# Decay rows in sample state homes, deferred outputs and a down tile in two banks in a decoder-trunk kernel

## The chip, the cores and the metric

The kernel runs on one core of one Trainium2 chip. The metric is the device time of one execution in microseconds (us). Before the change it is 991.7 us, the median of three runs (991.33 to 992.5).

The engines are called as in the profile: PE (TensorE, matmuls; PEld are its weight loads), DVE (VectorE), ACT (ScalarE), POOL (GpSimd), and SP (SyncE), which here only issues DMAs. A line number such as L928 is a line of the kernel before.

## The reference

One inference step of a decoder trunk: an FFN taken at half weight, a mixer, and a second FFN at half weight, each behind an RMS norm and with a residual add, then a last RMS norm. There are 512 prompt tokens and 8 sample tokens, 520 columns in all, and the model dimension is 1024. All data is float32.

```python
h = h + 0.5 * swiglu(rms_norm(h, n1), wg1, wu1, wd1)          # FFN dimension 2816
m, ... = mixer(rms_norm(h, nm), ...)
h = h + m
h = h + 0.5 * swiglu(rms_norm(h, n2), wg2, wu2, wd2)
y = rms_norm(h, final)
```

The mixer projects to a pooling part, a gate z, and x, B, C and dt of a Mamba-2 state-space scan (SSD). x, B and C go through a causal convolution over four tokens and SiLU. The scan works in chunks of 128 tokens, per head (16 heads in 2 groups, head size 64, state size 128):

```python
Acs = cumsum(dt * A)                                          # within a chunk
decay = exp(mask(Acs[l] - Acs[s]))
y_diag = (C[l] . B[s]) * decay * dt[s] * x[s]                 # summed over s
states = B[s] * exp(Acs[-1] - Acs[s]) * dt[s] * x[s]          # summed over s
y_off = C[l] . h_prev * exp(Acs[l])
y = y_diag + y_off + d_skip * x
```

The sample tokens read and update given states. Besides the two outputs y, the new pooling, convolution and SSD states are returned.

## The kernel before, in words

**Layout.** The 1024 features lie in eight tiles of 128 partitions with 520 columns each; a matmul takes half of the columns (260). To keep float32 precision each product is three matmuls of rounded parts, high by high, high by low, low by high (`mm3`, L116 to L121). A weight unit is loaded by SP, ACT casts the high part (L107), DVE subtracts for the low part (L108).

**FFN.** FFN1's down projection ends with `down` (L352 to L392): for each of the eight output tiles d it multiplies into a pair of PSUM banks (tag `BE`, two such pairs), and `done` takes both halves out with one DVE instruction (L369), adds them to h (L376) and calls `after`, which prepares that tile of the mixer's input (ACT L138, DVE L139, square and sum L149, L150). Tag `A` is two single banks that the gate and up products use.

**Mixer.** PSUM is then given anew as eight single banks (`bank`). The mixer opens with the `dt` product (L636 to L642), which goes over the two halves and, inside, over the eight input tiles. Its work is then cut into steps that two strings order, `CONV_PLAN` and `GATE_PLAN` (L39 to L46): b and x are projections with convolution (`conv`, L698), p, c and m the pooling (projection and window sums, `centre` L751, `mix` L760), A and B the two halves of a chunk step, z the gate's projections (`zproj`), s the sample tokens, e the stores of the small states (`outs_a`), o, G, H, g and h the gating and the output projection.

There are eight chunk steps: the four chunks of head group 0, then those of group 1, so A4 is chunk 0 of group 1, "the fifth". `ssd_a` (L860) does this for one step: it transposes B (`pb`) and four tiles of x (`px`, L871) on PE; loads the step's eight rows of cumulated decay from DRAM, each spread over 128 partitions (`ab`, L873, 512 KB); POOL makes `we`, the decay to the chunk's end (L877), and ACT its exponential (L878); for later chunks ACT makes `E`, the exponential of the rows (L883), and `cd` (L885); ACT (L888) and DVE (L890) subtract for four heads each, ACT exponentiates (L892, L893), all in place, and DVE multiplies with the masked scores `scm` (L899). DVE makes `xdt`, x times the step size dt, out of the bank `px` (L895), and POOL `xw` (L898). `ssd_b` (L902) multiplies (`yo`, `pst`, `yd`), brings the state up to date (`hst`, L920 and L921), adds up (L924, L925) and writes the output into x (L928, four instructions).

**Buffers.** `ab` has three buffers, `E`, `cd`, `xdt` and `we` two. Tag `h0` is four buffers of 2 KB per partition: first `dv` and `bct`, later the sample states that `sample` (L809) loads ("sample state homes").

**What sets the order.** A planner orders each engine's instructions at build time: it plays the program against modelled durations, and gives an engine, among the instructions that are ready by the model, the one traced first. `tc.high_priority()` puts what is traced inside ahead of others; `tc.issue_after(i)` keeps what is traced inside behind instruction i on i's engine; `tc.keep_in_program_order` pins an instruction behind what was traced before it on its engine. On the chip each engine then runs its list strictly in order, SP's DMA issues too, and waits by semaphore for data and for buffers and banks to come free.

## Time and profile before

| what | value |
|---|---|
| median of three runs | 991.7 us |
| profiled execution, its own time | 992.8 us |
| profiled execution, its span (first to last instruction) | 991.0 us |
| PE busy | 969.8 us |
| DVE busy | 800.0 us |
| ACT busy | 552.8 us |
| POOL busy | 87.4 us |
| read from HBM, written | 105.86 MB, 7.34 MB |

The profile is one execution. A row of a timeline gives the start in us from the span's start, the duration in us, the engine, the line, the operation, the names of what it writes and reads (`out<-in`), shapes, and how many instructions the row merges (x). In brackets stands how long the engine was idle before it, and which engine, name and line ended that. Where several semaphores were waited for, the one that came last is named. A matmul's end is modelled and overlaps the next one's start, so the distance of two starts is the better measure. By the core's rows, FFN1 ends and the mixer begins near 366 us, and the chunk steps lie between 426 and 561.

### The profile page before, as it was taken

The page shows a single profiled execution, that of the slowest core. Times are in us where ns is not written, and L with a number is a line of the kernel's source. Part 1 is how long each engine was busy: PE and PEld are TensorE (multiplying, and loading weights), DVE is VectorE, ACT ScalarE, POOL GpSimd, SP SyncE. Part 2 cuts the span into 40 slices and gives each one's busy share as a digit, 9 for nine tenths or more (in the row PEclk, how much of TensorE's full clock was granted, in tenths as well). Part 3 has the DMA queues.
Part 4 walks back from the last instruction along what each step waited for, and adds up shares of the span by engine and source line. Part 5 has one row for each costly group of instructions (what it writes and reads, how often), then busy time and mean ns, then how long its engine had stood idle before and what let it go on. Part 6 is the DMA issues. An engine that isn't in the chain of part 4 may idle for free.

```text
span 991.0 us, 19414 instructions
## 1 busy us (share of the span) xinstructions
PE 969.8 (98%) x7852; PEld 951.0 (96%) x7852; DVE 800.0 (81%) x1295; ACT 552.8 (56%) x1011; POOL 87.4 (9%) x157
## 2 busy tenths in 40 slices
PE   7999999999999999999999999999999999999996
PEld 6899999999999999999899999899999999999995
DVE  7999656997569688788978997999967899668876
ACT  7566414664136455685668574666643566534653
POOL 0000000000000000156522000100013000120000
PEclk9999999999999999999999999999999999999998
DMA  6332322323222232262335232323246423363212
GB/s 188 121 128 95 120 86 86 128 86 129 85 86 81 91 126 85 82 206 100 124 114 186 81 125 86 113 98 128 100 117 198 162 88 127 120 181 119 96 65 87
DMA packets 42027, 114.48 MB, mean 116 GB/s; under 512 B 6408, under 2 KB 13512, under 8 KB 41936
## 3 DMA queue, kind: packets, MB, share of 16 engines
q1 hardware_dynamic: 38864, 103.78, 30.6%
q0 software_dynamic: 3072, 9.44, 3.7%
q8 instruction: 62, 1.02, 0.4%
q14 instruction: 29, 0.24, 0.1%
HBM read 105.86 MB, written 7.34 MB: 114 GB/s over the span
## 4 chain that ended last, share of the span: by engine, by line
PE 90%; DVE 5%; POOL 1%; DMA 1%; issue 1%; ACT 1%; SPq 0%; DVEq 0%; ACTq 0%
PE A L121 8%; PE A L117 8%; PE A L120 8%; PE dn L121 7%; PE dn L117 7%; PE dn L120 7%; PE BE L117 6%; PE BE L121 6%; PE BE L120 6%; PE wo L117 2%; PE wo L121 2%; PE wo L120 2%; PE P L234 2%; PE inz L117 2%; PE inz L121 2%; PE inz L120 2%
## 5 line engine op out<-in xcount | busy, mean ns | idle before, releaser
L117 PE MATMUL dn<-g,whi_1d 128*128 128x260 f32 x352 | 99.3, 283 | 0.2 <-DVE td L369 0.2
L120 PE MATMUL dn<-g,whi_1d 128*128 128x260 f32 x352 | 99.5, 283 | 0.0
L121 PE MATMUL dn<-g,wlo_1d 128*128 128x260 f32 x352 | 99.4, 283 | 0.0
L369 DVE SCALAR_TENSOR_TENSOR td<-dn,r_f 128x520 f32<-128x520 f32 x40 | 27.8, 698 | 72.7 <-PE dn L121 72.7
L121 PE MATMUL dn<-g,wlo_2d 128*128 128x260 f32 x256 | 72.5, 283 | 0.8 <-DVE wlo_2d L108 0.8
L117 PE MATMUL dn<-g,whi_2d 128*128 128x260 f32 x256 | 72.3, 282 | 0.0
L120 PE MATMUL dn<-g,whi_2d 128*128 128x260 f32 x256 | 72.3, 282 | 0.0
L117 PEld LDWEIGHTS dn<-g,whi_1d 128*128 128x128 f32 x352 | 66.1, 188 | 0.4 <-DVE td L369 0.4
L120 PEld LDWEIGHTS dn<-g,whi_1d 128*128 128x128 f32 x352 | 66.3, 188 | 0.0
L121 PEld LDWEIGHTS dn<-g,wlo_1d 128*128 128x128 f32 x352 | 66.2, 188 | 0.0
L299 ACT COPY ac<-A 128x260 f32<-128x260 f32 x123 | 45.6, 374 | 28.9 <-PE A L121 28.0
L107 ACT CAST whi_1d<-raw_1d 128x1024 fp32r<-128x1024 f32 (+1 forms) x24 | 23.5, 981 | 67.0 <-PE dn L120 54.2
L262 DVE TENSOR_TENSOR s<-raw 128x1024 f32<-128x1024 f32 x41 | 49.9, 1218 | 5.6 <-DMA raw<-in_w2gu 5.6
L234 PE MATMUL P<-xg_f,raw 128*128 128x260 f32 x192 | 45.4, 392 | 6.4 <-ACT sq_f L157 5.5
L121 PEld LDWEIGHTS dn<-g,wlo_2d 128*128 128x128 f32 x256 | 48.2, 188 | 1.0 <-DVE wlo_2d L108 1.0
L234 PEld LDWEIGHTS P<-xg_f,raw 128*128 128x128 f32 x192 | 36.9, 196 | 12.2 <-ACT sq_f L157 5.4
L117 PEld LDWEIGHTS dn<-g,whi_2d 128*128 128x128 f32 x256 | 48.3, 189 | 0.0
L120 PEld LDWEIGHTS dn<-g,whi_2d 128*128 128x128 f32 x256 | 48.2, 188 | 0.0
L117 PE MATMUL wo<-catg,whi_wo 128*128 128x260 f32 x128 | 37.2, 290 | 0.0
L117 PE MATMUL inz<-xh_mx,whi_inz 128*128 128x260 f32 x128 | 36.8, 287 | 0.1
L117 PE MATMUL inx<-xh_mx,whi_inx 128*128 128x260 f32 x128 | 36.4, 284 | 0.0
L121 PE MATMUL wo<-catg,wlo_wo 128*128 128x260 f32 x128 | 36.2, 283 | 0.0
(1341 smaller groups left out, 3936.7 us busy)
## 6 DMA issues: line engine op xcount, KB each, us to landing
raw<-in_w2gu SPq DMA_DIRECT2D x44, 512.0 KB, 4.5
raw<-in_w1gu SPq DMA_DIRECT2D x42, 512.0 KB, 4.5
raw_1d<-in_w1d SPq DMA_DIRECT2D x16, 512.0 KB, 4.5
raw_2d<-in_w2d SPq DMA_DIRECT2D x16, 512.0 KB, 4.4
raw_wo<-in_w_out SPq DMA_DIRECT2D x12, 512.0 KB, 4.9
ab<-scr_acs SPq DMA_DIRECT2D x8, 512.0 KB, 4.9
h<-in_state_ssm SPq DMA_DIRECT2D x16, 256.0 KB, 3.7
raw_inz<-in_w_in SPq DMA_DIRECT2D x8, 512.0 KB, 3.8
```

What stands on the lines that cost most here:

```text
L107: nc.scalar.copy(h, src)
L117: first = nc.tensor.matmul(ps, whi, xhi, start=start, stop=False, **kw)
L120: nc.tensor.matmul(ps, whi, xlo, start=False, stop=False, **kw)
L121: nc.tensor.matmul(ps, wlo, xhi, start=False, stop=stop, **kw)
L234: nc.tensor.matmul(self.banks[f, u][b][:, :HB], ws(self.raw[f][:, u], j + 4 * q), xg[:, slot[q]], start=j == q == 0, stop=j == 3 and q == ...
L262: nc.vector.tensor_tensor(out=s1, in0=diag, in1=up0, op=ALU.add)
L299: nc.scalar.copy(keep, out[:, :HB])
L369: nc.vector.scalar_tensor_tensor(out=t, in0=banks[d][:, :, :HB], scalar=-0.5, in1=self.nx[3].rearrange("p (b t) -> p b t", b=2), op0=ALU.mult,
```

## The change

What it does, part by part:

- The last down tile of FFN1 (d = 7) multiplies into two single banks of tag `A` instead of a pair of tag `BE`, and is taken out half by half, at high priority (`done_by_half`). The `dt` product goes over the input tiles outside and the halves inside.
- The rows of the fifth step (chunk 0 of group 1) go into two buffers of tag `h0`, four heads each, with two DMAs of 256 KB. The lists of heads (`G`) and the products with `scm` follow.
- In every step, `xdt` is traced behind the transposes, at high priority. `we` is made on DVE instead of POOL, for the fifth step in two instructions. `E` and `cd` have three buffers.
- The output of step B1 (`ssd(1)`) is put off to a new step `Y1` behind A3, kept behind A3's `xdt` on DVE. Step `c3` moves behind B2, also kept behind A3's `xdt`.
- The stores of the small states (`e0`) move from the end of `CONV_PLAN` behind A5, and are kept behind A5's load of rows on SP.

```diff
-    "c3 X1 m2 A3 B2 e0"
+    "X1 m2 A3 Y1 B2 c3"
...
-    "A4 z0 B3 z1 m3 z2 B4 z3 s2 A5 z4 s2 B5 ...
+    "A4 z0 B3 z1 m3 z2 B4 z3 s2 A5 e0 z4 s2 B5 ...
...
+                    if after is not None and d == KD - 1:
+                        banks[d] = [ps[0].tile([P, 512], F32, tag="A", bufs=2, name=f"dn{self.i}_{d}_{c}{b}")
+                                    for b in range(2)]
...
+            def done_by_half(d):
+                for b, hs in enumerate(HALVES):
+                    t = self.wx.tile([P, 2, HB], F32, tag="tg", bufs=2, name=f"td{self.i}_{d}_{c}{b}")[:, b]
+                    nc.vector.scalar_tensor_tensor(out=t, in0=banks[d][b][:, :HB], scalar=-0.5, in1=self.nx[3][:, hs],
+                                                   op0=ALU.mult, op1=ALU.mult)
+                    nc.vector.tensor_tensor(out=h[:, d, hs], in0=t, in1=h[:, d, hs], op=ALU.add)
+                    after(d, b, hs)
...
-    for b, hs in enumerate(HALVES):
-        for k in range(KD):
+    for k in range(KD):
+        for b, hs in enumerate(HALVES):
...
+        if (c, g) == (0, 1):
+            abs_ = [mp.tile([P, 4, P], F32, tag="h0", bufs=4, name=f"ab{c}{g}{i}") for i in range(2)]
+            ab = None
+        else:
+            ab = mp.tile([P, 8, P], F32, tag="ab", bufs=3, name=f"ab{c}{g}")
+            abs_ = [ab]
+        n = 8 // len(abs_)
+        for i, t in enumerate(abs_):
+            r0 = c * NH + 8 * g + n * i
+            held["ab"] = nc.sync.dma_start(out=t, in_=scr_acs[r0 : r0 + n].unsqueeze(0).to_broadcast([P, n, P]))
...
+        xdt = mp.tile([P, 8, 64], F32, tag="xdt", bufs=2, name=f"xdt{c}{g}")
+        with tc.high_priority():
+            held["xdt"] = nc.vector.tensor_tensor(out=xdt, in0=px.rearrange("p (a b) -> p a b", a=8),
+                                                  in1=dtc.unsqueeze(2).to_broadcast([P, 8, 64]), op=ALU.mult).ins
...
-        nc.gpsimd.tensor_tensor(out=we, in0=ab[:, :, CH - 1], in1=atc, op=ALU.subtract)
+        for i, t in enumerate(abs_):
+            s = slice(n * i, n * i + n)
+            nc.vector.tensor_tensor(out=we[:, s], in0=t[:, :, CH - 1], in1=atc[:, s], op=ALU.subtract)
...
-            E = mp.tile([P, 4, P], F32, tag="E", bufs=2, name=f"E{c}{g}")
+            E = mp.tile([P, 4, P], F32, tag="E", bufs=3, name=f"E{c}{g}")
...
+        for t in abs_:
+            nc.vector.tensor_tensor(out=t, in0=t, in1=scm.unsqueeze(1).to_broadcast([P, n, P]), op=ALU.mult)
...
+        if (c, g) == ssd(1):
+            held["out"] = out
+        else:
+            out()
+
+    def ssd_out(_):
+        with tc.issue_after(held["xdt"]):
+            held.pop("out")()
...
     def outs_a():
+        with tc.issue_after(held["ab"].ins):
+            for name, t in (("ncp", ncp), ("ncs", sconv), ("npp", npp), ("nps", spool)):
+                nc.sync.dma_start(out=outs[name], in_=t)
+
+    def centre(j):
+        with tc.issue_after(held["xdt"]) if j == 3 else nullcontext():
+            pooled[j][0]()
```

More of the change, by code (lines that the diff above doesn't have):

```diff
@@ L358, in part @@
                     units[d] = load_unit(ins[f"w{self.i}d"][d, :, lo * P : hi * P], n * P, f"{self.i}d{d}_{c}")
-                    banks[d] = ps[0].tile([P, 2, 512], F32, tag="BE", bufs=2, name=f"dn{self.i}_{d}_{c}")
+                    if after is not None and d == KD - 1:
+                        banks[d] = [ps[0].tile([P, 512], F32, tag="A", bufs=2, name=f"dn{self.i}_{d}_{c}{b}")
+                                    for b in range(2)]
+                    else:
+                        t = ps[0].tile([P, 2, 512], F32, tag="BE", bufs=2, name=f"dn{self.i}_{d}_{c}")
+                        banks[d] = t[:, 0], t[:, 1], t
                 wh, wl = units[d]
@@ L368, in done @@
                 hd = h[:, d].rearrange("p (b t) -> p b t", b=2)
-                nc.vector.scalar_tensor_tensor(out=t, in0=banks[d][:, :, :HB], scalar=-0.5,
+                nc.vector.scalar_tensor_tensor(out=t, in0=banks[d][2][:, :, :HB], scalar=-0.5,
                                                in1=self.nx[3].rearrange("p (b t) -> p b t", b=2), op0=ALU.mult,
@@ L391, in down @@
                 part(d, range(n))
-                done(d)
+                if after is not None and d == KD - 1:
+                    with tc.high_priority():
+                        done_by_half(d)
+                else:
+                    done(d)
         def down_by_half(self, c, lo, after, wd):
@@ L914, in ssd_b @@
             nc.tensor.matmul(yd[64 * (q % 2) : 64 * (q % 2) + 64, (q // 2) * P : (q // 2 + 1) * P], xdt[:, q],
[L915 removed]
+                             G[q], start=True, stop=True)
         if c == 0:
@@ L926, in ssd_b, with out @@
             yr = E
-        for q in range(4):
-            nc.vector.scalar_tensor_tensor(out=X[:, 4 * g + q, cs], in0=X[:, 4 * g + q, cs],
-                                           scalar=v("d_skip", 4 * g + q), in1=yr[:, q], op0=ALU.mult, op1=ALU.add)
+        def out():
+            for q in range(4):
+                nc.vector.scalar_tensor_tensor(out=X[:, 4 * g + q, cs], in0=X[:, 4 * g + q, cs],
+                                               scalar=v("d_skip", 4 * g + q), in1=yr[:, q], op0=ALU.mult, op1=ALU.add)
+        if (c, g) == ssd(1):
+            held["out"] = out
+        else:
+            out()
+    def ssd_out(_):
+        with tc.issue_after(held["xdt"]):
+            held.pop("out")()
     zbox = []
@@ L994, in outs_a @@
     def outs_a():
-        nc.sync.dma_start(out=outs["ncp"], in_=ncp)
-        nc.sync.dma_start(out=outs["ncs"], in_=sconv)
-        nc.sync.dma_start(out=outs["npp"], in_=npp)
-        nc.sync.dma_start(out=outs["nps"], in_=spool)
+        with tc.issue_after(held["ab"].ins):
[4 more added lines that the diff above has]
+            pooled[j][0]()
     stages = {
```

30 lines of the change are left out of this document (14 added, 16 removed).

## The prediction

> **What bounds the kernel now.** I read the page first, then TensorE's list of waits, then the timelines of single engines around each wait.
>
> ```profile
> PE 969.8 (98%) x7852; PEld 951.0 (96%) x7852; DVE 800.0 (81%) x1295; ACT 552.8 (56%) x1011; POOL 87.4 (9%) x157
> PE 90%; DVE 5%; POOL 1%; DMA 1%; issue 1%; ACT 1%; SPq 0%; DVEq 0%; ACTq 0%
> ```
>
> TensorE (PE) is busy for 98% of the span and holds 90% of the chain that ended last. The change takes no matmul away, so it can only win where TensorE stands still. Those places are few. In the list of TensorE's waits (who waits, on whom, total us, times, longest):
>
> ```profile
> PE P L234 <- ACT sq_f L157: 5.5, 1, 5.5
> PE dt L640 <- DVE td L369: 0.9, 1, 0.9
> ```
>
> The longest belongs to the prologue, which the diff does not touch. The second, and three shorter ones at L914, L863 and L871, lie in its reach. They are two places: the hand-over from the last down tile to `dt`, and one stretch near 480 us. The timeline of TensorE shows both; the last number in brackets is the idle time before the row:
>
> ```profile
> 365.99 0.28 PE L121 MATMUL dn<-g,wlo_1d 128*128 128x260 f32 x1
> 367.16 0.29 PE L640 MATMUL dt<-xh_mx,w 128*48 128x260 f32 x1 [0.88 <-DVE td L369]
> 367.29 0.28 PE L642 MATMUL dt<-xl_mx,w 128*16 128x260 f32 x1
> ...
> 477.57 1.02 PE L911 MATMUL pst<-xw,bt 128*128 128x512 f32 x2
> 478.99 1.09 PE L914 MATMUL yd<-ab,xdt 128*64 128x128 f32 x16 [0.40 <-DVE U L622]
> 480.66 0.30 PE L863 MATMUL pb<-ident,BC 128*128 128x128 f32 x1 [0.58 <-DVE U L624]
> 481.84 0.55 PE L871 MATMUL px<-ident,X 128*128 128x128 f32 x3 [0.66 <-DVE xdt L895]
> 482.44 0.39 PE L117 MATMUL inz<-xh_mx,whi_inz 128*128 128x260 f32 x1
> ```
>
> All four are waits for a PSUM bank that VectorE (DVE) has not yet emptied. At 480 us the kernel's eight banks are all in use, and VectorE is late with all of them: it empties the conv step x7's first half (`U`, L622) at 478.52, though the matmuls of that half had ended before the `pm`, `pb`, `px`, `yo` and `pst` matmuls that stand ahead of `yd`. So the question is what VectorE did instead:
>
> ```profile
> 473.17 0.69 DVE L921 TENSOR_TENSOR hst<-pst,hst 128x512 f32<-128x512 f32 x1 [0.34 <-POOL hst L920]
> 473.77 2.61 DVE L928 SCALAR_TENSOR_TENSOR X<-X,h,E 128x128 f32<-128x128 f32 x4
> 477.08 1.52 DVE L890 TENSOR_SCALAR ab<-ab,tok 128x128 f32<-128x128 f32 x2 [0.70 <-ACT E L883]
> 478.52 0.42 DVE L622 TENSOR_TENSOR U<-inx,r_mx 128x260 f32<-128x260 f32 x1
> 478.86 1.25 DVE L890 TENSOR_SCALAR ab<-ab,tok 128x128 f32<-128x128 f32 x6
> 480.36 0.15 DVE L624 TENSOR_TENSOR U<-inx,r_mx 128x8 f32<-128x8 f32 x1
> 480.43 0.75 DVE L753 SCALAR_TENSOR_TENSOR PW<-PW,PU 128x497 f32<-128x497 f32 x2
> 481.11 0.67 DVE L895 TENSOR_TENSOR xdt<-px,tok 128x512 f32<-128x512 f32 x1
> ```
>
> (The last number but the bracket is how many instructions the row merges.) It wrote the outputs of chunk step B1 (L928, 2.61 us), stood 0.70 for ScalarE's `E`, ran the decay differences (L890) of two chunk steps at once, centred the fourth pool group (L753), and only then reached `xdt`. The other engines, ScalarE (ACT), GpSimd (POOL) and the DMA queue of SyncE (SP), say why:
>
> ```profile
> 476.42 1.28 ACT L883 ACTIVATE E<-ab 64x512 f32<-64x512 f32 x2 [3.04 <-DVE X L928]
> ```
>
> ```profile
> 473.09 2.62 POOL L742 TENSOR_TENSOR PW<-PW 128x652 f32<-128x652 f32 x2
> 476.61 0.20 POOL L877 TENSOR_TENSOR we<-ab,tok 128x8 f32<-128x8 f32 x1 [0.90 <-DMA ab<-scr_acs]
> ```
>
> ```profile
> 470.45 0.38 SPq L998 DMA_DIRECT2D out_nps<-spool  x1
> 470.88 0.42 SPq L873 DMA_DIRECT2D ab<-scr_acs  x1
> 482.10 9.55 SPq L873 DMA_DIRECT2D ab<-scr_acs  x2
> ```
>
> ScalarE waited 3.04 us for L928, because `E` has two buffers and B1's outputs still read one. GpSimd waited for the fifth step's decay rows, issued at 470.88 behind the state store of L998; the sixth and seventh steps' went out from 482.10 on.
>
> **The change part by part.** *Last down tile in two banks; dt loop.* The tile d = 7 moves from the double bank (tag BE) to the two single banks (tag A), which FFN1's last gate tile has left. I infer that `dt`'s first banks then lie over tile 5's double bank, which is free one whole tile earlier. The start of `dt` moves from 367.16 to one pitch (0.13, the step from 367.16 to 367.29) after 365.99: 367.16 - 365.99 - 0.13 = **1.04 us**. What is late next is tile 7's own input to `dt`, k = 7. With k outermost, 28 of 32 matmuls come before it: 28 x 0.13 = 3.6 us, until 369.7. The chain from the tile's end at 366.3 has these steps:
>
> ```profile
> 366.31 0.70 DVE L369 SCALAR_TENSOR_TENSOR td<-dn,r_f 128x520 f32<-128x520 f32 x1
> 367.27 1.23 DVE L108 TENSOR_TENSOR wlo_inbc<-raw_inbc,whi_inbc 128x1024 fp32r<-128x1024 f32 x1 [0.26 <-ACT whi_inbc L107]
> 368.41 0.76 DVE L376 TENSOR_TENSOR h<-td,h 128x260 f32<-128x260 f32 x2
> 369.41 0.49 DVE L139 SCALAR_TENSOR_TENSOR xl_mx<-h,xh_mx 128x260 fp32r<-128x260 f32 x1 [0.21 <-ACT xh_mx L138]
> ```
>
> By halves, and with the first half done while the second multiplies, half of 0.70, half of 0.76, some 0.7 for ScalarE's `xh` (from the adds' end 369.17 less half an add to 369.41, rounded up) and 0.49 end near 368.3; the weight split of 1.23 no longer stands between, by the high priority. That leaves 1.4 us. Were the split still between, the chain would end at 369.5, just in time. So the gain lies between 0 and 1.04, and I take 1.04. One more instruction pair on VectorE is hidden under matmuls.
>
> *The stretch at 480 us.* Its full price comes from the same sequence without waits, one step on:
>
> ```profile
> 518.87 1.02 PE L911 MATMUL pst<-xw,bt 128*128 128x512 f32 x2
> 521.59 0.36 PE L117 MATMUL inz<-xh_mx,whi_inz 128*128 128x260 f32 x1
> ```
>
> From `pst` to the first `inz`, 2.72 us without waits; 482.44 - 477.57 = 4.87 with them. The difference is **2.15 us**; the idle alone is 0.40 + 0.58 + 0.66 = 1.64. Four edits work on it. (1) `E` and `cd` in three buffers: ScalarE's 3.04 and VectorE's 0.70 go. (2) B1's four outputs go behind step A3's `xdt` (`Y1`): 2.61 leaves the front of x7's halves. (3) `c3`'s centring goes behind the same point: 0.75. (4) `xdt` is traced early and at high priority, so it follows its transposes. Together 0.70 + 2.61 + 0.75 = 4.06 us leave the queue ahead of `xdt`, which started at 481.11; the emptying of x7's halves moves ahead by 0.70 + 2.61 = 3.31, to 475.2 and 477.1. `yd` wants its bank when `pst` ends at 477.57 + 1.02 = 478.6 and `pb` 1.09 later at 479.7; both are then free, and `xdt`, at 481.11 - 4.06 = 477.1, ends at 477.8, before `px` wants to start. Late next are `yo`'s and `pm`'s banks, which `inz` needs from 477.57 + 2.72 = 480.3 on; the first is emptied by the `E` product (L924), the next in VectorE's queue behind `xdt`, as long as no other work is put ahead of it.
>
> What the edits cost: `we` moves from GpSimd to VectorE, 9 instructions of 128x8 (the fifth step has two). The nearest row is L624 at 0.15, so 1.4 us over eight steps, of which some fall before 482; the gain on the other side is that L890 and L888 no longer wait for GpSimd. The fifth step's product with `scm` becomes two instructions, 0.15 more. The work moved is not gone: 2.61 and 0.75 now fall into 477 to 503. There VectorE has little room:
>
> ```profile
> 482.40:505.00 22.60, 22.56 (x187) 20.88 (x189) 21.54 (x45) 18.11 (x38) 5.33 (x6) 1.00 0.30 100
> 449.68 1.12 DVE L928 SCALAR_TENSOR_TENSOR X<-X,h,yd 128x128 f32<-128x128 f32 x4
> ```
>
> (Columns: window, sum, busy PE, weight loads, DVE, ACT, POOL.) VectorE has 22.60 - 21.54 = 1.1 us free in this window, and 0.34 + 0.70 = 1.04 of waiting ahead of it that can be filled. The four outputs took 1.12 us elsewhere, so 1.5 of the 2.61 was something else than their work. I take the 2.15 in full, less 0.2 for a leftover wait; bounds 0 and 2.15.
>
> [...]
>
> *Rows of the fifth step in two sample state homes; stores later.* The two 256-KB loads need no `ab` buffer, so they can go out with the first three steps' rows instead of at 470.88, in place of two of the early state loads:
>
> ```profile
> 426.25 1.79 SPq L813 DMA_DIRECT2D h<-in_state_ssm x3
> ```
>
> The sixth step's rows take the buffer that the fifth had, free once B1's `yd` is done, which is also what let the fifth's go by 470.88; so they can go out near 470 instead of 482.10. SP issues one DMA more, some 0.4. The stores wait for GpSimd's last copies of x7; with `issue_after` they stand behind the sixth step's rows. What SP has queued behind a waiting store are weights of later `z` steps, which it loads two units ahead, and the seventh step's rows. I cost it at nothing, and bound it by the seventh rows' own wait, the 9.55 us that merge the two loads at 482.10, within which TensorE lost nothing.
>
> **The sum.** Against the profiled execution, 992.8 (span 991.0 and 1.8 around it): -1.04 - 2.15 + 0.2 = -3.0, so 989.8. The median of the three runs, 991.7, stands 1.1 below the profiled one; there it gives **988.7 us**.
>
> **The rivals.**
> *VectorE only shifts its lag (0.17).* For it: 95% busy after 482.4, 1.1 us free, and 3.4 us of work moved into that window. The banks that `inz` and the next `yo` need are then late instead. Against it: TensorE did not wait there before, while VectorE was as late. Then only the 1.04 stays: 990.7.
> [...]
> *VectorE stands at the head for a load: slower (0.07).* `we` is now VectorE's first touch of the rows, in order, and it waits for the DMA. For the sixth step the rows were seen landing here:
>
> ```profile
> 486.07 0.22 ACT L885 ACTIVATE cd<-ab 128x8 f32<-128x8 f32 x1 [0.38 <-DMA ab<-scr_acs]
> ```
>
> If the rows still leave at 482.10 and the planner puts their `we` right behind A3's `xdt`, near 478, VectorE stands 8 us with every bank full behind it: 988.7 + 8 = 996.7. It decides against the change from a stand of 3 us on, and is slower by over 0.2% from 5. Against it: the buffer is free from about 470.
> *The homes are not free (0.03).* If sample states still take all four homes early, the fifth step's rows wait until the samples are read, issued no sooner than:
>
> ```profile
> 519.00 2.07 SPq L813 DMA_DIRECT2D h<-in_state_ssm x2
> ...
> 504.57 1.09 PE L914 MATMUL yd<-ab,xdt 128*64 128x128 f32 x16
> ```
>
> B4's `yd` would be over 519.0 - 504.6 = 14 us late and the time about 1003. Against it: the fifth step is traced ahead of the samples.
>
> **How the numbers follow.** Forecast 0.64, rivals 0.17, 0.09, 0.07 and 0.03. The forecast alone is faster by over 0.2% (2.0 us, about what a measurement of this kernel can tell from no change): 0.64. The shifted lag and the port are within it: 0.26. The last two are slower: 0.10. The low end takes both gains in full, 988.5, less the 0.8 that the runs of before lie from their median at most (992.5 against 991.7): 987.7. The high end is no gain at all plus 0.3 of cost, 992.0. Both slower cases stay outside, 1 in 10.
>
> **What would show it.** Right: no wait of `dt` on `td`; `U` of x7 emptied by 477 and none of the waits of `yd`, `pb` and `px` near 480 left; no wait of ScalarE's `E` on L928 there; the rows of the fifth step issued before 430, of the sixth near 470. Wrong: new TensorE waits on `zs` (L938), `E` or `pm` between 480 and 505; VectorE idle before `we` on a DMA; `we` over 1 us; VectorE's weight splits later than TensorE needs them. A planner that orders a distant stage anew, say the second FFN's opening, would make the sum wrong without making a step wrong.

## The result, and the profile after

The changed kernel took 996.13 us (median of six runs, 994.84 to 996.69), the kernel before 991.66 in the same job (six runs, 991.05 to 992.5). The ratio is 1.0036, with a 95% interval of 1.0026 to 1.0047. That is 3.6 us slower (the two medians lie 4.5 apart), where 3.0 faster was forecast, and above the high end of the range, 992.0. The profiled execution of the changed kernel is its fastest, 994.84 with a span of 992.9, so the profiles show 1.9 us of the loss. What the slower executions add is in no profile.

In the rows below, line numbers are those of the kernel that is shown; the names carry over (the differences of the decay rows, L890 before, are L922 after; `xdt` L895 is L904, `U` L622 is L639, the outputs L928 are L962, GpSimd's window sums L742 are L759).

The page first: TensorE's busy time went up by 1.3 us with the same matmuls, and its share of the chain fell from 90% to 75%.

```profile
PE 971.1 (98%) x7852; PEld 952.1 (96%) x7852; DVE 800.7 (81%) x1306; ACT 554.9 (56%) x1013; POOL 79.7 (8%) x149
PE 75%; issue 11%; DVE 7%; DMA 3%; ACT 2%; SPq 1%; POOL 0%; DVEq 0%; POOLq 0%; ACTq 0%
```

Where the time went is best seen in windows that are cut at TensorE's own landmarks: from FFN1's first gate product to the first `inbc` (the first projection behind `dt`), from there to the first `inz` (the stretch at 480 us lies at its end), from there to the first `wo`, and the rest. Columns: window, length, busy PE, weight loads, DVE, ACT, POOL, the granted TensorE clock, DMA share, GB/s. Before:

```profile
36.91:371.64 334.73, 333.64 (x2774) 332.67 (x2773) 257.03 (x372) 162.85 (x260) 0.72 (x3) 1.00 0.30 104
371.64:482.44 110.80, 109.12 (x913) 105.39 (x911) 92.27 (x184) 71.67 (x133) 43.89 (x90) 1.00 0.36 123
482.44:542.56 60.12, 60.12 (x508) 56.40 (x508) 49.97 (x101) 45.82 (x126) 13.57 (x12) 1.00 0.42 139
542.56:991.04 448.48, 436.33 (x3532) 430.55 (x3530) 371.68 (x597) 246.46 (x460) 28.97 (x50) 0.99 0.36 116
```

After:

```profile
36.17:370.31 334.14, 333.66 (x2774) 332.61 (x2773) 256.95 (x373) 162.86 (x261) 0.72 (x3) 1.00 0.31 105
370.31:483.41 113.10, 109.26 (x912) 105.61 (x910) 91.41 (x185) 76.48 (x140) 40.44 (x85) 1.00 0.38 125
483.41:545.00 61.59, 61.40 (x510) 57.48 (x509) 52.28 (x112) 42.79 (x119) 10.53 (x8) 0.98 0.39 128
545.00:992.90 447.90, 436.27 (x3532) 430.48 (x3530) 370.94 (x595) 246.67 (x460) 27.80 (x50) 0.99 0.35 116
```

The first window is 0.59 shorter: that is the down tile's part. The second is 2.30 longer, where 1.95 less was forecast (2.15, with 0.2 taken off for a leftover wait). The third is 1.47 longer with nearly the same matmuls, at a clock of 0.98 instead of 1.00. The rest, and the start (36.17 instead of 36.91), give 0.58 and 0.74 back, in stages that the change does not touch. Sum: -0.74 - 0.59 + 2.30 + 1.47 - 0.58 = +1.86, the difference of the spans (1.88) but for rounding.

TensorE's waits, and its timeline near 480 us:

```profile
PE px L888 <- DVE catp L783: 2.0, 1, 2.0
PE yd L946 <- DVE U L639: 1.9, 1, 1.9
...
PE dt L657 <- DVE td L374: 0.3, 1, 0.3
```

```profile
476.37 1.02 PE L943 MATMUL pst<-xw,bt 128*128 128x512 f32 x2
479.26 1.09 PE L946 MATMUL yd<-ab,xdt 128*64 128x128 f32 x16 [1.87 <-DVE U L639]
...
482.82 0.90 PE L888 MATMUL px<-ident,X 128*128 128x128 f32 x3 [1.97 <-DVE catp L783]
483.41 0.58 PE L117 MATMUL inz<-xh_mx,whi_inz 128*128 128x260 f32 x1
483.79 0.42 PE L120 MATMUL inz<-xl_mx,whi_inz 128*128 128x260 f32 x1
...
485.95 0.28 PE L121 MATMUL inz<-xh_mx,wlo_inz 128*128 128x260 f32 x1
```

Two waits of 1.9 and 2.0 us stand where three with 1.64 in sum stood. Right behind them a matmul takes 0.42 instead of 0.28 until 485.9: the granted clock is at one half for 3.41 us, from 482.5 on.

```profile
482.40:485.90 3.50, 3.08 (x14) 2.99 (x15) 3.50 (x8) 0.97 (x4) 1.08 (x1) 0.52 0.31 103
```

VectorE, ScalarE, GpSimd and SP in that stretch:

```profile
473.97 0.67 DVE L953 TENSOR_TENSOR hst<-pst,hst 128x512 f32<-128x512 f32 x1
474.57 1.11 DVE L909 TENSOR_TENSOR we<-ab,tok 128x4 f32<-128x4 f32 x2
475.71 3.16 DVE L922 TENSOR_SCALAR ab<-ab,tok 128x128 f32<-128x128 f32 x4
478.79 0.42 DVE L639 TENSOR_TENSOR U<-inx,r_mx 128x260 f32<-128x260 f32 x1
...
481.13 1.23 DVE L108 TENSOR_TENSOR wlo_inz<-raw_inz,whi_inz 128x1024 fp32r<-128x1024 f32 x1 [1.51 <-ACT whi_inz L107]
482.28 0.48 DVE L783 SCALAR_TENSOR_TENSOR catp<-pm,h,catp 128x260 fp32r<-128x260 f32 x1
482.68 0.67 DVE L904 TENSOR_TENSOR xdt<-px,tok 128x512 f32<-128x512 f32 x1
```

```profile
475.63 0.69 ACT L920 ACTIVATE ab<-ab,tok 128x128 f32<-128x128 f32 x2 [6.02 <-DVE we L909]
...
480.07 1.03 ACT L107 CAST whi_inz<-raw_inz 128x1024 fp32r<-128x1024 f32 x1
```

```profile
474.31 4.28 POOL L759 TENSOR_TENSOR PW<-PW 128x652 f32<-128x652 f32 x3
```

```profile
423.55 2.54 SPq L899 DMA_DIRECT2D ab<-scr_acs  x5
...
472.15 0.38 SPq L899 DMA_DIRECT2D ab<-scr_acs  x1
```

The five loads from 423.55 on are three steps' rows and the two halves of the fifth's, which went out before 430 as forecast; the sixth step's followed at 472.15 (near 470 was forecast). Step B1's outputs have left the front of x7's halves, as planned. In their place stand the fifth step's `we` and differences, whose rows now lie ready early: 4.27 us instead of the 2.61. ScalarE no longer waits for `E`; it stands 6.02 for `we` instead, with the weight cast `whi_inz` and the evacuation of `pm` queued behind. VectorE then stands 1.51 for `whi_inz`, and `xdt`, although traced early and at high priority, comes behind.

### The profile page after: what moved, and what is told of

Its sections match the earlier page's. It is cut to its first block, busy times and chain, and to the rows that moved or that the text cites. A ratio compares the mean times of both kernels' runs of the same rounds, so it can differ in the third digit from the quotient of the medians.

```text
span 992.9 us, 19413 instructions
## 1 busy us (share of the span) xinstructions
PE 971.1 (98%) x7852; PEld 952.1 (96%) x7852; DVE 800.7 (81%) x1306; ACT 554.9 (56%) x1013; POOL 79.7 (8%) x149
## 4 chain that ended last, share of the span: by engine, by line
PE 75%; issue 11%; DVE 7%; DMA 3%; ACT 2%; SPq 1%; POOL 0%; DVEq 0%; POOLq 0%; ACTq 0%
PE A L121 6%; PE A L120 6%; PE A L117 6%; PE dn L117 6%; PE dn L121 6%; PE dn L120 6%; PE BE L117 5%; PE BE L121 5%; PE BE L120 5%; PE wo L117 2%; PE wo L121 2%; PE wo L120 2%; PE P L234 2%; PE inz L117 1%; PE inz L120 1%
## 5 line engine op out<-in xcount | busy, mean ns | idle before, releaser
L120 PE MATMUL inz<-xl_mx,whi_inz 128*128 128x260 f32 x128 | 36.7, 287 | 0.0
L121 PE MATMUL inz<-xh_mx,wlo_inz 128*128 128x260 f32 x128 | 36.5, 286 | 0.0
```

What stands on the lines that cost most here:

```text
L120: nc.tensor.matmul(ps, whi, xlo, start=False, stop=False, **kw)
L121: nc.tensor.matmul(ps, wlo, xhi, start=False, stop=stop, **kw)
```

## The experiments

Eighteen kernels were run beside the kernel before, each timed against it on the same chip. The table sets them side by side. The two lengths are those of the windows above (first `inbc` to first `inz`, first `inz` to first `wo`), in each kernel's profiled execution; "waits" are TensorE's waits of 0.2 or more between 470 and 500 us, "half clock" is how long the granted clock was 0.5 there.

| kernel | ratio to before, 95% interval | inbc to inz | inz to wo | waits | half clock |
|---|---|---|---|---|---|
| before | | 110.80 | 60.12 | 0.4, 0.6, 0.7 | 0 |
| changed | 1.0036, 1.0026 to 1.0047 | 113.10 | 61.59 | 1.9, 2.0, 0.2 | 3.4 |
| 1 last tile only | 0.9989, 0.9980 to 0.9997 | 110.62 | 60.12 | 0.4, 0.7 | 0 |
| 2 changed, rows in `ab` | 1.0049, 1.0037 to 1.0061 | 114.80 | 61.94 | 1.3, 4.5 | 6.8 |
| 3 changed, `we` on GpSimd | 1.0019, 1.0010 to 1.0027 | 112.00 | 62.78 | 0.7, 2.2, 0.2 | 6.8 |
| 4 changed, `we` behind x7 | 1.0032, 1.0020 to 1.0043 | 113.35 | 62.03 | 4.3 | 6.8 |
| 5 tile and early rows | 0.9986, 0.9977 to 0.9995 | 110.08 | 60.19 | 0.9 | 0 |
| 6 tile and `we` on VectorE | 0.9998, 0.9990 to 1.0007 | 110.04 | 61.63 | 0.4, 0.5, 1.3 | 0 |
| 7 tile and early `xdt` | 0.9989, 0.9980 to 0.9997 | 110.11 | 60.12 | 0.3, 0.7 | 0 |
| 8 tile and later stores | 1.0041, 1.0028 to 1.0054 | 112.69 | 62.21 | 0.4, 2.3, 0.6 | 6.8 |
| 9 changed, stores back | 1.0040, 1.0027 to 1.0052 | 112.77 | 61.60 | 1.7, 2.0 | 3.4 |
| 10 as 9, `we` on GpSimd | 1.0030, 1.0019 to 1.0042 | 112.36 | 61.50 | 0.9, 2.2 | 3.4 |
| 11 tile, E, outputs, centring, `xdt` | 1.0053, 1.0039 to 1.0066 | 114.25 | 62.41 | 1.0, 4.3 | 6.8 |
| 12 tile, rows, `xdt`, three E | 1.0017, 1.0008 to 1.0027 | 112.73 | 60.03 | 1.5, 2.0 | 0 |
| 13 changed, no sums | 1.0036, 1.0023 to 1.0050 | 112.11 | 61.46 | 3.1, 0.7, 0.2 | 0 |
| 14 before, no sums | 0.9988, 0.9979 to 0.9996 | 110.22 | 60.28 | 1.3 | 0 |
| 15 tile, rows, `xdt`, centring | 1.0015, 1.0006 to 1.0024 | 111.01 | 60.12 | 0.2, 1.6 | 0 |
| 16 as 15, sums on VectorE | 0.9980, 0.9971 to 0.9989 | 109.04 | 60.87 | 0.5 | 0 |
| 17 changed, E and cd later | 1.0039, 1.0026 to 1.0052 | 112.75 | 62.11 | 1.7, 2.0 | 6.8 |
| 18 as 17, sums on VectorE | 0.9986, 0.9977 to 0.9995 | 110.78 | 60.15 | 1.3, 0.4 | 0 |

The theory at the start: what is new ahead of x7's halves, the fifth step's early work, makes the whole loss. Its rival: each part is harmless or good alone, and the loss is a matter of which engine stands at its queue's head for something late.

**1. The last down tile alone.** The kernel before with the first two parts of the diff (two single banks for d = 7, `dt` by input tiles outside).

> The kernel before with the last down tile in two banks and the dt loop alone. My theory of the loss (the fifth step's early decay work stands ahead of x7's emptying on VectorE and ScalarE) has no part in it, so it keeps the gain of the hand-over: dt's 0.88 us wait falls to 0.3 or less and the time is 0.7 to 1.0 us under the kernel before, near 990.8. Rival (the tile's edit itself sets back something later): 992 or more.

It gained 1.1 us (0.3 to 2.0). In the profile, first gate product to first `inbc` is 334.13 against 334.73, so 0.60; the stretch keeps two of its three waits (that of `yd` falls under 0.2). This part stands on its own, and its gain is in all the kernels below that have it.

**2, 3 and 4. The changed kernel with the fifth step's early work hindered in three ways.** Rows back in the third `ab` buffer; `we` back on GpSimd; `we` of the fifth step kept behind x7's emptying.

```diff
-        if (c, g) == (0, 1):
-            abs_ = [mp.tile([P, 4, P], F32, tag="h0", bufs=4, name=f"ab{c}{g}{i}") for i in range(2)]
...
```

> The changed kernel with the fifth step's rows back in an ab buffer, one load; all else kept. Theory (early rows let the planner put the fifth step's work ahead of x7's first half): x7's first half is emptied by about 475, yd waits under 0.5 us, the granted clock stays full, 990 to 991.5. Rival 'we on VectorE': ScalarE still stands some 6 us for we and the time stays 995 to 996. Rival 'outputs and centring put off': 994 to 996, with the waits on E or catp.

```diff
-            nc.vector.tensor_tensor(out=we[:, s], in0=t[:, :, CH - 1], in1=atc[:, s], op=ALU.subtract)
+            nc.gpsimd.tensor_tensor(out=we[:, s], in0=t[:, :, CH - 1], in1=atc[:, s], op=ALU.subtract)
```

> The changed kernel with we back on GpSimd in all steps; rows still early. Theory: the four differences of the fifth step still stand ahead of x7's first half and beside the pool sums, so yd still waits 1 us or more; without we's 1.1 us on VectorE the time falls a little, 993 to 995. Rival 'we on VectorE is the cause': no such wait, 989 to 990.

```diff
...
-            nc.vector.tensor_tensor(out=we[:, s], in0=t[:, :, CH - 1], in1=atc[:, s], op=ALU.subtract)
+            with tc.issue_after(held["U"]) if (c, g) == (0, 1) else nullcontext():
+                nc.vector.tensor_tensor(out=we[:, s], in0=t[:, :, CH - 1], in1=atc[:, s], op=ALU.subtract)
```

> The changed kernel with the fifth step's we (and so its differences) kept behind the emptying of x7's second half on VectorE; rows still early, we still on VectorE, outputs still put off. Theory: the waits of yd and px fall under 0.5 us in sum, the clock stays full, 989 to 990. Rival 'we on VectorE holds ScalarE': ScalarE waits as long or longer, the px wait stays near 2 us, 993 or more. Rival 'outputs put off': 993 or more.

None came back to the forecast: 1.0049, 1.0019, 1.0032. Kernel 3's time lies in the 993 to 995 that its theory gave, but its long wait is at `px` (2.2) and not at `yd` (0.7); kernel 2 came out above all its ranges, and kernel 4 where its rivals had it. So the theory in its first form falls. In the second kernel VectorE stood 3.08 us for the rows' DMA ahead of `we`. In the fourth x7's halves were empty in time and the wait of `yd` was gone, but ScalarE now stood for the sixth step's rows, its `cd` being queued ahead of `whi_inz`:

```profile
479.85 1.28 ACT L918 ACT_TABLE_LOAD   x1 [9.72 <-DMA ab<-scr_acs]
481.14 0.21 ACT L918 ACTIVATE cd<-ab 128x8 f32<-128x8 f32 x1
481.26 1.03 ACT L107 CAST whi_inz<-raw_inz 128x1024 fp32r<-128x1024 f32 x1
```

One stand taken away, another ended at the same place, and TensorE waited 4.3 instead of 3.8 in sum.

**5 to 8. One part each, on top of the last tile.** Only the early rows; only `we` on VectorE; only the early `xdt`; only the later stores (each with its lines of the change's diff).

> The kernel before with the new last down tile, and the fifth step's decay rows in two sample homes (early); `we` stays on GpSimd, `E` and `cd` keep two buffers, outputs, centring, `xdt` and stores as before. Theory (the early rows pull the fifth step's work ahead of x7's emptying, and with it an engine stands at its queue's head): the stretch at 480 us gets waits of TensorE of 2 us or more and a halved clock for 3.4 us: 993 to 996. Rival (the rows alone are harmless, since `we` on GpSimd has its own place): as the last-tile kernel alone, 991, stretch waits 0.5 to 1.7 us in sum, no halved clock.

> The kernel before with the new last down tile, and `we` of all steps on VectorE; all else as before. Theory (`we` on VectorE puts VectorE itself behind the rows' landing, issued at 471 to 472 us, and ScalarE behind it): VectorE idle 1 us or more before `we` on a DMA near 476, x7's halves emptied 1 us later or more: 992 to 995, halved clock if a wait of TensorE passes 2 us. Rival (`we` is 0.15 us and its place does not matter): 991, waits as before.

> The kernel before with the new last down tile, and `xdt` traced right behind its transposes at high priority. Theory (this part is harmless or helps): 990 to 991.2; the wait of `px` on `xdt` near 481.8 (0.66) goes or shrinks, the waits of `yd` and `pb` stay. Rival (its place ahead of other work of VectorE makes the halves of x7 or the decay differences late): 991.5 to 994, a wait of `yd` or `pb` over 1 us.

> The kernel before with the new last down tile, and the four state stores issued behind the sixth step's rows. Theory (SP's place alone: the fifth step's rows no longer stand behind stores that wait for GpSimd, so they land earlier, and nothing is put ahead of x7's halves): GpSimd's 0.90 wait for the rows goes, `E` on ScalarE and the first half of x7 up to 0.9 earlier: 990 to 991. Rival (SP's buffer waits for weights hold them as long anyway): 991, waits in the stretch as before. Second rival (the stores then delay weights of `z` steps): waits of TensorE on weights between 490 and 520, 992 or more.

Early rows and early `xdt` cost nothing and gain at most half a microsecond (110.08 and 110.11 against 110.62), which the intervals of the times do not resolve. `we` on VectorE takes the tile's gain back, by a wait of 1.3 for the SiLU of x further on. (Its time, 992.4, lies in the range that its theory gave, by luck: VectorE did not stand for the rows as that theory said.) The later stores alone make 1.0041, and by none of the three ways that were on record: GpSimd's `we` no longer stands between its sums, and all three remaining sums run in one piece beside VectorE's outputs. The kernel with the later stores, GpSimd and VectorE:

```profile
472.05 4.24 POOL L759 TENSOR_TENSOR PW<-PW 128x652 f32<-128x652 f32 x3
```

```profile
472.73 3.97 DVE L945 SCALAR_TENSOR_TENSOR X<-X,h,E 128x128 f32<-128x128 f32 x4
```

(Kernel 6 has the same 3.98 and survives it, since six of its eight differences run before x7's halves; in kernel 8 four of them, 1.83 us, come behind the centring and right ahead of `xdt`, which `px` then waits for.) The same four outputs took 1.12 elsewhere and 2.61 beside two sums; beside three they take 3.97. So the price moves with the sums, 0.75 us for each of two and 0.95 for each of three, and not with the outputs. That is the second theory: **GpSimd's window sums hold VectorE by a fixed amount, and whatever stands beside them pays it.** Before, the outputs paid 2.61 - 1.12 = 1.5 and the first two differences, 1.52 beside the third sum against 0.47 alone (kernel 5), 1.0; after, `we` and the four differences pay 3.2. So the amount is fixed only roughly. And not all that stands beside the sums pays: in kernel 4 VectorE takes x7's halves out of their PSUM banks beside three sums in 0.41 and 0.40 us (the first took 0.42 before), and the differences behind them take 3.18.

**9 to 12. Are the stores, or the three buffers, the culprit?** The changed kernel with the stores in their old place; the same with `we` on GpSimd; the last tile with only `E`, outputs, centring and `xdt`; the last tile with rows, `xdt` and three buffers of `E` and `cd`.

```diff
-    "X1 m2 A3 Y1 B2 c3"
+    "X1 m2 A3 Y1 B2 c3 e0"
...
```

> The changed kernel with the four state stores back in their old place (stage e0 behind B2, no issue_after); all other parts of the change stay. Theory (moving the stores is what loses: it lets the sixth step's rows and its products come ahead, so that VectorE and ScalarE put decay work ahead of what TensorE waits for): 988.5 to 990.5, no wait of TensorE over 1 us near 480 and no halved clock there. Rival (the early rows, `we` and the deferred outputs lose together, whatever the stores do): 994 to 997 with a wait of 1.9 us or more near 480 and the clock at 0.5 for 3.4 or 6.8 us.

> The changed kernel with the stores in their old place and `we` back on GpSimd; rows early, outputs and centring deferred, `xdt` early, three buffers of `E` stay. Theory (stores lose, `we` on VectorE costs up to 1.3 by a wait of the first z step's transposes): 988.5 to 990, at most the time of the kernel with the stores alone put back. Rival (deferring the outputs moves the lag to TensorE's later waits): 991 to 993, waits of `px`, `inz` or `yo` between 482 and 505 us of 1 us or more.

> The kernel before with the new last down tile, `E` and `cd` in three buffers, the outputs of B1 and the centring deferred, and `xdt` early; rows, `we` and stores as before. Theory (these four edits do what the sum of 2.15 said, if nothing else is moved): 988.5 to 990, waits of `yd`, `pb`, `px` near 480 under 0.3 in sum. Rival (with `E` in three buffers the planner draws the fifth step's work ahead of x7's emptying, and its rows, issued at 471, hold VectorE): 992 to 996 with a wait over 1.9 us.

> The kernel before with the new last down tile, early rows of the fifth step in two sample homes, `xdt` early and `E` and `cd` in three buffers; `we` on GpSimd, outputs, centring and stores as before. Theory: ScalarE's 3.04 us wait for `E` goes, which lets the fifth step's work fill idle time: 989 to 990.5. Rival (the outputs of 2.6 us beside GpSimd's sums still stand ahead of x7's halves): 990.5 to 991.5, with a wait of `yd`, `pb` or `px` of 0.5 to 1 us left.

All four lose, so the stores are one way to the loss and not the only one. Kernel 9 came out as its rival said, the other three above both of their ranges. In kernel 12 the outputs (2.96) and the fifth step's differences (2.21) stand together beside the sums, ahead of x7's first half. Kernel 11 tells most of the prediction, since it is just the four edits that were to bring 2.15. Here VectorE first stood 3.09 us for GpSimd's `we`, which waited for the fifth step's rows, issued at 470.99; that is the rival on record, and `pb` waited 1.0 for it. Then the deferred outputs came where the banks for the first z unit were to be emptied, beside GpSimd's next work, and cost 2.70 there:

```profile
476.77 2.14 DVE L911 TENSOR_SCALAR ab<-ab,tok 128x128 f32<-128x128 f32 x4 [3.09 <-POOL we L898]
...
479.83 2.70 DVE L947 SCALAR_TENSOR_TENSOR X<-X,h,E 128x128 f32<-128x128 f32 x4
482.46 0.75 DVE L770 SCALAR_TENSOR_TENSOR PW<-PW,PU 128x497 f32<-128x497 f32 x2
483.12 1.21 DVE L108 TENSOR_TENSOR wlo_inz<-raw_inz,whi_inz 128x1024 fp32r<-128x1024 f32 x1
484.26 0.47 DVE L783 SCALAR_TENSOR_TENSOR catp<-pm,h,catp 128x260 fp32r<-128x260 f32 x1
```

```profile
PE inz L117 <- DVE catp L783: 4.3, 1, 4.3
```

The 3.4 us that left the front of `xdt` stand ahead of the weight split and the evacuation of `pm`, and `inz` waits 4.3. How much of this the stand of 3.09 made and how much the outputs was not taken apart.

**13 and 14. Without the sums.** One fill with zeros stands for the four sums of the fourth pool group, in the changed kernel and in the kernel before.

```diff
+            if g == 3:
+                nc.gpsimd.memset(nxt, 0.0)
+                cur = nxt
+                break
```

> The changed kernel without the window sums of the fourth pool group (one fill with zeros on GpSimd stands for four sums, so that part of the pooling is left out). Theory (GpSimd's sums hold VectorE: 2.3 us in the changed kernel, whichever instructions stand beside them): the fifth step's four differences take 0.9 instead of 3.16 us, x7's halves are emptied 2 to 3 us earlier, no halved clock near 480: 989 to 991, about 5 below the changed kernel. Rival (the queue order and ScalarE's hold for `we` alone lose): waits of 2 us stay: 994 to 997.

> The kernel before without the window sums of the fourth pool group (as above, part of the pooling is left out). Theory (before loses the same 2.5 us of VectorE, 1.5 on the outputs and 1.0 on the first differences): the outputs take 1.1 instead of 2.6 us, the waits at 480 fall from 1.64 to under 0.5: 990 to 991, 1 to 1.6 below before. Rival (the outputs are slow for another reason): 991.5 to 992.5 and outputs of 2.6 us.

The hold is shown: without the sums the changed kernel's four differences take 0.86 instead of 3.16, and x7's first half is empty 4.6 us earlier, both counted from the first `pm` behind x7. Before's outputs take 1.12 (2.61 with the sums), and that kernel gains the 1.2 us that were forecast, though a wait of 1.3 is left, now at `inz`. But the changed kernel's time stays at 1.0036, as the rival on record had it. VectorE is free, and then stands for ScalarE, which stands for the sixth step's rows; these went out only at 472.57, behind the weights of a z unit:

```profile
475.18 0.86 DVE L926 TENSOR_SCALAR ab<-ab,tok 128x128 f32<-128x128 f32 x4
...
480.93 1.23 DVE L108 TENSOR_TENSOR wlo_inz<-raw_inz,whi_inz 128x1024 fp32r<-128x1024 f32 x1 [4.49 <-ACT whi_inz L107]
```

```profile
479.75 0.21 ACT L921 ACTIVATE cd<-ab 128x8 f32<-128x8 f32 x1 [1.63 <-DMA ab<-scr_acs]
479.87 1.03 ACT L107 CAST whi_inz<-raw_inz 128x1024 fp32r<-128x1024 f32 x1
```

So the changed kernel has two stands that end close together: the sums, through VectorE's `we` and ScalarE's wait for it, and the sixth step's rows. Counted from the first `pm` behind x7, ScalarE's `cd` runs 5.97 us after it in the changed kernel, where no wait for the rows shows, and 5.15 after it in kernel 13, where it waited for them. Either stand alone is enough for over 3 us of waiting.

**15 and 16. What a version without these stands gives.** The last tile, early rows, early `xdt`, and the centring behind B2, with two buffers of `E`; and the same with the fourth group's sums on VectorE.

```diff
-            nc.gpsimd.tensor_tensor(out=nxt[:, lo:LP], in0=cur[:, lo:LP], in1=cur[:, lo - step : LP - step], op=ALU.add)
+            (nc.vector if g == 3 else nc.gpsimd).tensor_tensor(out=nxt[:, lo:LP], in0=cur[:, lo:LP], in1=cur[:, lo - step : LP - step], op=ALU.add)
```

> The kernel before with the new last down tile, early rows of the fifth step, `xdt` early, and the centring of the fourth pool group behind B2; `E` and `cd` in two buffers, outputs, `we` and stores as before. Theory (without the third buffer of `E` nothing of the fifth step gets in front, and the 0.75 of centring leaves the place ahead of `xdt`): the 0.9 wait of `px` falls to 0.2: 989.5 to 991, against 994.4 of the kernel with three buffers. Rival (early rows and early `xdt` lose together, whatever `E` has): 993 to 996, with a wait of 1.5 us or more near 480.

> As the kernel with early rows, early `xdt` and later centring on the new last down tile, with the four window sums of the fourth pool group on VectorE instead of GpSimd; nothing is left out. Theory (VectorE stood 2.5 us for GpSimd's sums anyway, and with sums of its own, some 0.75 us each, it loses no more and its order is its own): outputs 1.1 us, differences under 1.0, waits near 480 under 0.5 in sum: 989 to 990.5. Rival (four sums of 0.75, 3 us more work of VectorE, are late at x7's halves): a wait of `yd` over 1 us: 991 to 994.

Kernel 15 missed its forecast; its time, 993.6, and its wait of 1.6 are those of its rival. The wait on `xdt` fell from 0.9 to 0.2 as expected, but the centring, moved behind `xdt`, met GpSimd's `xw` there and took 1.61 instead of 0.75, ahead of the `E` product whose bank `inz` wants: 1.6 of waiting. Again the price moved along. Early rows and early `xdt` without the later centring were not run, so that the two alone lose together is not ruled out. Kernel 16 is the best of all: 0.9980, 2.0 us under before (1.1 to 2.9 less). Sums on VectorE take 0.82 each, and nothing stands beside them:

```profile
474.94 1.13 DVE L959 SCALAR_TENSOR_TENSOR X<-X,h,E 128x128 f32<-128x128 f32 x4
475.99 0.82 DVE L759 TENSOR_TENSOR PW<-PW 128x640 f32<-128x640 f32 x1
```

Its window from `inbc` to `inz` is 109.04, so 1.76 of the 2.15 that the prediction read from the stretch is really there to be had, but not by the change's means; 0.75 of it is given back in the next window (60.87 against 60.12).

**17 and 18. The two stands of the changed kernel, one and both.** `E` and `cd` of the sixth step are kept behind the evacuation of `pm` on ScalarE; then the sums also move to VectorE. All parts of the change stay.

```diff
+            after_mix = (c, g) == (1, 1)
...
-            nc.scalar.activation(out=cd, in_=ab[:, :, CH - 1], func=AF.Exp)
+            with tc.issue_after(held["mix"]) if after_mix else nullcontext():
+                nc.scalar.activation(out=cd, in_=ab[:, :, CH - 1], func=AF.Exp)
```

> The changed kernel whose sixth step's `E` and `cd` on ScalarE are kept behind the evacuation of `pm` of the third pool group, so that ScalarE doesn't stand for that step's rows ahead of the weight cast of the first z unit. Theory (two holds end together, GpSimd's sums on VectorE's side and the sixth step's rows on ScalarE's; taking one away leaves the other): VectorE still loses some 3 us to the sums, ScalarE still stands 6.0 us for `we`: 994 to 997, waits of 1.9 and 1.9 us as in the changed kernel. Rival (ScalarE's hold for the rows is the whole cause): 989 to 991.

> As the kernel above, and the four window sums of the fourth pool group on VectorE instead of GpSimd; nothing is left out, all parts of the change stay. Theory (both holds gone): `we` of the fifth step at 473 to 474, its four differences 0.9 us, x7's halves emptied by 477, weight cast of the first z unit begun before 477.5, waits of TensorE near 480 under 0.5 in sum and no halved clock: 988.5 to 990.5. Rival (something else in the change loses, as the deferred outputs in front of what empties the banks for the first z unit): a wait of 1 us or more of `px` or `inz`, 992 or more.

With ScalarE's stand alone mended nothing changes (1.0039, the same two waits), as forecast. With both, the loss is gone: 0.9986, which is 0.0050 or 5 us under the changed kernel's ratio, and the clock stays whole. `we` takes 0.22, the differences 0.86:

```profile
474.70 0.22 DVE L909 TENSOR_TENSOR we<-ab,tok 128x4 f32<-128x4 f32 x2
...
477.32 0.86 DVE L925 TENSOR_SCALAR ab<-ab,tok 128x128 f32<-128x128 f32 x4
478.11 0.81 DVE L759 TENSOR_TENSOR PW<-PW 128x640 f32<-128x640 f32 x1
478.84 0.41 DVE L639 TENSOR_TENSOR U<-inx,r_mx 128x260 f32<-128x260 f32 x1
```

My 988.5 to 990.5 was too low all the same: a wait of 1.3 of `yd` is left, since VectorE's own sums and differences now stand ahead of x7's halves. Its window is 110.78, just as before the change, so the gain that is left is the tile's. The four tests around the changed kernel read: both stands 113.10, the rows alone 112.11, the sums alone 112.75, none 110.78. Two things keep this from being a clean square. Kernel 13 leaves the sums out where kernel 18 moves them, and in kernel 18 SP also sent the sixth step's rows earlier, at 468.84 instead of 472.15. The changed kernel with only the sums moved was not run, so whether the edit on ScalarE was needed stays open.

## Why the prediction was wrong

**The last tile: right, mis-sized.** The term was 1.04; the changed kernel and kernel 1 show 0.59 and 0.60 (334.14 and 334.13 against 334.73). The start of `dt` did come forward by 1.06. The step that was too good is the inference that both its banks are free a tile earlier. With the halves inside, the second matmul pair goes to the other bank at once, and that one waits for tile 7's own second half:

```profile
365.48 0.28 PE L659 MATMUL dt<-xl_mx,w 128*16 128x260 f32 x1
366.05 0.32 PE L657 MATMUL dt<-xh_mx,w 128*48 128x260 f32 x1 [0.28 <-DVE td L374]
```

366.05 - 365.48 less a pitch of 0.12 is 0.45, and 1.04 - 0.45 = 0.59. The input of tile 7, which I had feared as the next to be late, had its room.

**The stretch: the step that failed is "together 4.06 us leave the queue ahead of `xdt`".** Of the 2.61 for the outputs only 1.12 was their own work. The prediction said so itself and still subtracted all 2.61. The hold belongs to GpSimd's sums, which stayed; with `we` gone from between them they ran in one piece of 4.28 us, where before two took 2.62 and the third came later. The hold passed to the next instructions, `we` and the differences: 1.11 + 3.16 against 0.22 + 0.86 with the sums on VectorE (kernel 18), 3.2 us. VectorE began to empty x7's first half at 478.8 and not at 475.2.

**No term at all: the early rows.** Rows that lie ready let the planner put the fifth step's `we` and differences ahead of x7's halves. Alone, with two buffers of `E`, that costs nothing (kernel 5). Together with what else the change frees, it fills the place that the outputs left.

**"Costed at nothing": the stores.** On top of the tile they lose 5.2 us by themselves (1.0041 against 0.9989, kernels 8 and 1); there too the three sums run in one piece. In the changed kernel, where `we` has left GpSimd anyway, putting them back gains nothing (kernel 9).

**"ScalarE's 3.04 goes": what was late next was not asked.** ScalarE's next instruction was one that waits for `we`, 6.02 us, and behind that one for the sixth step's rows (9.72 in kernel 4). The cast `whi_inz` is behind both. It began 5.0 us after the first `pm` behind x7 before (480.17, `pm` at 475.18), and 6.1 after it in the changed kernel (480.07, 473.99), where VectorE then stood for it.

**"It follows its transposes": the high priority did not do it.** `xdt` ran behind the split `wlo_inz`, which stood 1.51 for `whi_inz`. How the planner's model came to that order is not shown; whether three buffers of `E` alone are enough for it was not run by itself.

**Not in the sum at all: the clock.** Of the third window's 1.47, about 1.3 is TensorE at half speed behind the waits (busy 61.40 against 60.12 us); 0.2 is a wait of `px` for `X`.

**The rivals.** "The port" stands in the chances with 0.09, as a case within 2.0 us of no change. No run shows a port. What the runs show is that VectorE loses time beside GpSimd's sums, at a price of 3.2 on VectorE, and this turned a gain into a loss, where I had let it give back a gain at most. "VectorE only shifts its lag" is a part of what kernel 11 shows, again with a loss (4.3) where the rival ended at no gain. "VectorE stands at the head for a load" came near the measured time, 996.7, by luck: its reason did not decide in the changed kernel. It shows in kernel 2 (3.08 for a DMA), through GpSimd's `we` in kernel 11 (3.09) and, on ScalarE, in kernels 4 and 13. The range failed since its cases outside the slower ones were capped at "no gain": a wait that becomes longer than the one removed was never priced.

## What to carry to other kernels

What an instruction loses beside another engine's work need not go along when the instruction is moved. Here B1's outputs, 2.61 us beside the sums, left; `we` and the differences in their place took 4.27 against 1.08 in kernel 18, while x7's halves were emptied beside the same sums in 0.41 and 0.40 (kernel 4). Bound the hold by the holder's rows (3.2 of the sums' 4.28 us here), and subtract only the instruction's undisturbed duration (1.12 for the outputs). Where a change frees buffers or brings data early, ask for each queue which instruction will come to its head and what that one waits for, up to the first that TensorE needs: in kernel 4 ScalarE stood 9.72 us for `cd`'s rows, with `whi_inz` queued behind.

## What the runs showed of the hardware

Waits of TensorE had a second price. In the profiles the granted clock fell to 0.50 for 3.4 or 6.8 us behind waits in this stretch (the table's last column). Some kernels show it and others with similar waits do not. Two waits of 1.9 and 2.0 us, 1.6 us apart, stood ahead of it in the changed kernel; 3.1 and then 0.7 (kernel 13) and two of 1.5 and 2.0 (kernel 12) were followed by none, in the one profile of each. Waits of 1.7 and 2.0 stood ahead of 3.4 us of it in kernel 9 and of 6.8 in kernel 17.

The clock's own records in two traces give the lengths. In the changed kernel it is full for 474.45 us from its first rise on, half for 3.41 and full for 501.76, which is 139, 1 and 147 times 3.413; in the kernel before it is full for 976.21, 286 times as long. Cut from the first rise into stretches of that length, the changed kernel has TensorE idle for 1.83 us in the stretch ahead of the fall, and for 1.70 or less in all others at full clock but the last, at the kernel's end (3.39, with a fall behind it). In the kernel before it is 1.28 or less, but for the last (2.70, with a fall behind it). In the changed kernel's stretch at half clock TensorE was idle for 0.30, and the clock was full behind it. The last two stretches before the fall in the changed kernel, and the two that share kernel 13's wait of 3.1 (idle time is the length less the first number behind the comma):

```profile
475.69:479.10 3.41, 1.71 (x10) 0.88 (x8) 3.39 (x5) 2.91 (x7) 3.01 (x4) 1.00 0.63 222
479.10:482.51 3.41, 1.58 (x19) 1.22 (x19) 1.90 (x5) 3.41 (x8) 1.68 (x5) 1.00 0.35 109
```

```profile
477.74:481.15 3.41, 1.77 (x20) 1.22 (x19) 0.22 (x1) 1.78 (x4) 0.59 (x1) 1.00 0.61 210
481.15:484.57 3.42, 1.91 (x14) 1.68 (x15) 3.42 (x6) 1.37 (x4) 1.04 (x1) 1.00 0.13 52
```

The idle times are 1.70 and 1.83 in the changed kernel and 1.64 and 1.51 in kernel 13. So the longer wait of kernel 13, cut in two, left less idle time in either stretch than the two waits of the changed kernel left in the one ahead of the fall. That is what was measured; why the clock falls is not shown. The idle times rest on modelled ends of matmuls and are not exact to the hundredth.
